# Weights split on other engines, query and key blocks stored in halves, later oT transposes in a diffusion trunk

## The chip, the cores and the metric

The kernel runs on one core of a Trainium2 chip. The metric is the device time of one execution in microseconds. Three runs of the kernel before took 1909.53, 1918.72 and 1919.75 us; their median is 1918.72.

TensorE (PE in the profile) multiplies matrices, VectorE (DVE) and ScalarE (ACT) work on elements, GpSimd (POOL) too; SyncE (SP) issues most transfers. Each engine takes its own list of instructions in order.

## The reference, cut to what matters

The reference is a two-layer trunk over 1024 latent tokens of width 1024 with 256 context tokens. Layer 0 projects the normalised tokens once and splits the result among neighbourhood attention (8 heads of 64) and a bidirectional gated DeltaNet (4 heads of 128, chunks of 64), with a gate z over both. Layer 1 is a Hyena layer with long convolutions. The part that the change touches is layer 0's projection and the DeltaNet. Per head and direction:

```
kb, vb = k * beta[..., None], v * beta[..., None]
lmat = where(strict, (kb @ k.T) * decay, 0)
sol  = triangular_solve(lmat, concat[vb, kb * exp(gc)], unit lower)   # u, w
aqk  = (q @ k.T) * decay
scan over chunks: o = exp(gc) q @ S + aqk @ (u - w @ S);  S = decayed S + k.T @ (...)
```

The neighbourhood attention needs q, k and v of 8 heads (two heads, a "pair", in one block of 128 columns), laid out so that a window of columns is contiguous.

## The kernel before, in words

Every projection is a block of 128 output columns against all 1024 inputs. Precision is held by splitting each operand into a high and a low part: a block is three matmuls (high x high, high x low, low x high) for each of 8 slices of the input and each stretch of 512 tokens (`gemm`, `gemm_steps`). `load_split` loads the raw weights [128, 8 x 128], casts them to the high part and subtracts to get the low part (line 105). Before the change the cast is ScalarE's by default (line 102) or another engine's (line 104), and the subtraction GpSimd's. Two weight buffers of each kind take turns, so a part of one block may be written when the block before the last one is finished.

`project` has two stages. In stage 1 (385 to some 726 us of the span) a scheduler orders the instructions of each engine from dependences and its own costs. `dn_front` runs for four heads: three projections (`dn_block`: k, v, q; tiles dn and wdn), a centred convolution on VectorE (dacc), transposes (ktp, vtp, qtp), the norms of k and q (rk, rr), the scaled ktm and its transpose kT, and then, for each half of the chunks and each direction, the products kk and aq, the row R of decays, and the masked matrices W and Wi; W is stored in lsc. Names like R_4_1 mean the second half of the chunks (from chunk 4 of 8) and the second direction; groups 8, 0 and 4 follow each other. I call this last part a head's tail. Its banks (pool pst) are three. `dn_substitute` inverts diagonal 32x32 blocks on GpSimd in 31 steps (tiles sub and Xb, lines 755 and 757), with W reloaded as Lb, and stores the result in xsc; `dn_tiles` loads it as X and U; `dn_levels` combines the blocks with small matmuls (y_0_0, z_0_0, y_0_0_0, ...). Substitutions 0 and 1 and the levels of head 0 are in stage 1, as are the gate blocks z 4 to 7 and, through a filler, z 0 and 1 and q, k, v of pair 0 (nq, nk, nv).

In stage 2 (to 985 us) TensorE's order is that of the program. Each head's chunks are scanned (`dn_scan`: hops of pa<-vtm, pa<-vg,ktm, pa<-S,kT and the outputs pb, oacc), with a given number of filler matmuls between the hops: q, k and v of pairs 1 to 3 and z 2 and 3. `dn_finish` normalises oacc on VectorE and defers the transposes oT and the product with z (line 926): a deferred piece is issued after so many fillers. 40 fillers (FILL_LOAD) stand ahead of the scans of heads 1 to 3.

The query and key blocks of a pair go through staging tiles nvst: high and low part of all 1024 tokens, cast and subtracted from line 515 on, stored to nq_d and nk_d at line 523. In stage 1 these tiles are the two buffers that dpad uses otherwise, in stage 2 two of their own.

## Time and profile before

| | us |
|---|---|
| median of three runs | 1918.72 |
| profiled execution | 1915.67 |
| its span | 1913.7 |
| TensorE busy | 1743.7 (91%) |
| VectorE busy | 1379.5 (72%) |
| ScalarE busy | 853.8 (45%) |
| GpSimd busy | 624.6 (33%) |

TensorE's mean granted clock is 0.953 of full speed. The profiled execution's own time is 2.0 us more than its span. A busy engine is not yet the reason for the time: what counts is where TensorE stands idle or runs at a lower clock, and what ends that. An entry such as "[5.85 <-POOL wdn_lo L105]" says that the engine stood idle for 5.85 us and that GpSimd's instruction of line 105 that writes wdn_lo ended it.

### The profile page before, as it was taken

What the parts mean: (1) busy time and instruction counts of PE and PEld (TensorE: products, weight loads), DVE (VectorE), ACT (ScalarE), POOL (GpSimd) and SP (SyncE); (2) the same over time, 40 slices, a digit from 0 to 9 for tenths busy, and PEclk for the clock granted to TensorE, in tenths of its full rate; (3) what the DMA queues carried; (4) which work ended last, traced back from release to release, by engine and by line L of the source; (5) the groups of instructions that cost most, each with busy time, mean ns of one, the idle gap of its engine ahead of it and who ended that gap; (6) DMA issues with size and microseconds to landing.
All of it is one profiled execution on the core that took longest, in us unless ns stands there. A gap on an engine that the chain in (4) does not pass through costs nothing. (4 is left out here: it accounts for less than half of the span.)

```text
span 1913.7 us, 30399 instructions
## 1 busy us (share of the span) xinstructions
PE 1743.7 (91%) x11156; PEld 1422.0 (74%) x11156; DVE 1379.5 (72%) x2786; ACT 853.8 (45%) x1851; POOL 624.6 (33%) x878
## 2 busy tenths in 40 slices
PE   6798988799987998999988999888999999999998
PEld 2466755688876786888866787677888888888776
DVE  5999988657648544655565665748898998898666
ACT  5566564445525342333343544544344444444421
POOL 0755554412395767811044301420000000000310
PEclk9799978899999998999998999999999999999999
DMA  8445544313434367534389854533442443444424
GB/s 303 162 131 142 171 159 160 121 45 108 142 104 122 128 202 230 174 103 158 142 236 236 233 172 105 181 94 81 111 121 72 101 124 81 123 111 112 126 104 135
DMA packets 132080, 271.05 MB, mean 142 GB/s; under 512 B 43946, under 2 KB 65978, under 8 KB 129883
## 3 DMA queue, kind: packets, MB, share of 16 engines
q1 hardware_dynamic: 122330, 233.45, 37.8%
q0 software_dynamic: 9600, 35.66, 9.9%
q8 instruction: 88, 1.44, 0.3%
q14 instruction: 62, 0.50, 0.1%
HBM read 193.03 MB, written 76.03 MB: 141 GB/s over the span
## 5 line engine op out<-in xcount | busy, mean ns | idle before, releaser
L116 PE MATMUL hx<-h1h,w1x_hi 128*128 128x512 f32 x256 | 101.2, 395 | 0.0
L112 PE MATMUL dn<-hh,wdn_lo 128*128 128x512 f32 (+1 forms) x256 | 95.6, 375 | 5.9 <-POOL wdn_lo L105 5.9
L116 PE MATMUL hx<-h1l,w1x_hi 128*128 128x512 f32 x256 | 100.9, 394 | 0.0
L652 DVE SCALAR_TENSOR_TENSOR dacc<-dpad,convw,dacc 128x1024 f32<-128x1024 f32 (+1 forms) x80 | 83.8, 1078 | 23.6 <-ACT dacc L650 19.3
L116 PE MATMUL hx<-h1h,w1x_lo 128*128 128x512 f32 x256 | 100.7, 393 | 0.0
L111 PE MATMUL dn<-hl,wdn_hi 128*128 128x512 f32 (+1 forms) x256 | 95.2, 372 | 0.0
L110 PE MATMUL dn<-hh,wdn_hi 128*128 128x512 f32 (+1 forms) x256 | 95.2, 372 | 0.0
L757 POOL TENSOR_TENSOR Xb<-Xb,sub 80x31 f32<-80x31 f32 (+15 forms) x124 | 86.3, 696 | 8.4
L755 POOL TENSOR_TENSOR sub<-Lb,Xb 80x31 f32<-80x31 f32 (+15 forms) x124 | 76.0, 613 | 35.0 <-DMA Lb<-lsc_d 21.0
L1051 ACT ACTIVATE pr<-pr,st 128x640 f32<-128x640 f32 (+1 forms) x64 | 51.4, 802 | 63.6 <-DVE st L1050 63.5
L112 PEld LDWEIGHTS dn<-hh,wdn_lo 128*128 128x128 f32 x256 | 49.1, 192 | 14.7 <-POOL wdn_lo L105 6.1
L1171 ACT COPY fx<-fx_ps 128x512 f32<-128x512 f32 (+1 forms) x96 | 43.5, 483 | 28.4 <-PE fx_ps L121 24.9
L116 PE MATMUL hu<-h1h,w1u_lo 128*128 128x512 f32 x128 | 51.3, 401 | 4.7 <-DMA w1u_lo<-in_w 4.7
L110 PEld LDWEIGHTS dn<-hh,wdn_hi 128*128 128x128 f32 x256 | 49.2, 192 | 7.8
L121 PE MATMUL fx_ps<-ident,ff 128*128 128x128 f32 x288 | 49.9, 300 | 5.6 <-ACT fx L1171 3.6
L111 PEld LDWEIGHTS dn<-hl,wdn_hi 128*128 128x128 f32 x256 | 49.0, 192 | 8.0 <-issue 0.5
L116 PEld LDWEIGHTS hx<-h1h,w1x_lo 128*128 128x128 f32 x256 | 48.1, 188 | 9.0
L116 PEld LDWEIGHTS hx<-h1h,w1x_hi 128*128 128x128 f32 x256 | 48.2, 188 | 8.9
L116 PEld LDWEIGHTS hx<-h1l,w1x_hi 128*128 128x128 f32 x256 | 48.1, 188 | 8.9
L156 POOL DMA_DIRECT2D w1x_lo<-in_w x16 | 13.8, 864 | 124.8 <-ACT w1x_lo L154 116.7
L1280 PE MATMUL fh<-fhh,w3s 128*128 128x512 f32 x64 | 37.2, 584 | 16.6 <-DVE fh L1282 16.5
L116 PE MATMUL hu<-h1h,w1u_hi 128*128 128x512 f32 x128 | 51.5, 402 | 0.8 <-ACT hpu L1632 0.8
(571 smaller groups left out, 5967.4 us busy)
## 6 DMA issues: line engine op xcount, KB each, us to landing
hG<-g_d SPq DMA_DIRECT2D x16, 1088.0 KB
g_d<-G SPq DMA_DIRECT2D x16, 1024.0 KB
em_w<-in_em_w SPq DMA_DIRECT2D x24, 512.0 KB
om_w<-in_om_w SPq DMA_DIRECT2D x24, 512.0 KB
wz_raw<-in_w0z SPq DMA_DIRECT2D x16, 512.0 KB
w1x_raw<-in_w SPq DMA_DIRECT2D x16, 512.0 KB
w1x_lo<-in_w POOLq DMA_DIRECT2D x16, 512.0 KB, 8.0
wdn_raw<-in_w0dn SPq DMA_DIRECT2D x12, 512.0 KB
```

The lines of the kernel that those rows point to most:

```text
L110: nc.tensor.matmul(ps, wh, xh, start=start, stop=False)
L111: nc.tensor.matmul(ps, wh, xl, start=False, stop=False)
L112: nc.tensor.matmul(ps, wl, xh, start=False, stop=stop)
L116: ins = self.nc.tensor.matmul(*args, **kw)
L121: ins = self.nc.tensor.transpose(out, x, self.ident)
L156: nc.gpsimd.dma_start(lo, src, accum_op=ALU.add)
L652: nc.vector.scalar_tensor_tensor(acc[:, t0:t0 + n], pad[:, o + j:o + j + n], cw[:, blk, j:j + 1], acc[:, t0:t0 + n], ALU.mult, ALU.add)
L755: nc.gpsimd.tensor_tensor(tv, Lb[:, j + 1:, j:j + 1].broadcast_to([80, m, c]), Xb[:, j:j + 1, 0:c].broadcast_to([80, m, c]), ALU.mult)
L757: nc.gpsimd.tensor_tensor(Xb[:, j + 1:, 0:c], Xb[:, j + 1:, 0:c], tv, ALU.subtract)
L1051: nc.scalar.activation(pr[:, :n], pr[:, :n], AF.Exp, bias=st[:, 0:1], scale=-1.0, accum_out=st[:, 1:2])
L1171: nc.scalar.copy(out[:, j0:j0 + m, :].rearrange("p a b -> p (a b)"), ps[:, :m * P])
L1280: nc.tensor.matmul(ps, ws[:, od, :], hh[:, sl], start=True, stop=False)
```

## The change

Three things change.

First, `load_split` takes an engine for the low part. The twelve dn blocks and the four z blocks of stage 1 have it subtracted by VectorE instead of GpSimd. The five filler weights of stage 1 (z 0, z 1, and q, k, v of pair 0) have the high part cast by ScalarE instead of GpSimd and the low part subtracted by VectorE. The fillers of stage 2 keep both on GpSimd.

Second, query and key blocks are staged for 512 tokens at a time. Each half is cast, subtracted and stored on its own: four stores of 256 KB per block, in runs of 64 elements (256 bytes), where two stores of 512 KB had whole rows of 1024 elements. Stage 2 has four staging tiles of 512 columns for two of 1024; in stage 1 one dpad buffer holds both parts of a half. Values are written by two copies of 256 columns instead of one of 512.

Third, the transposes oT of heads 0 to 2 are issued 60 fillers after the head's end instead of 39, which is inside the next head's scan.

```diff
-            self.split(raw, hi, lo, hi_eng=hi_eng)
+            self.split(raw, hi, lo, hi_eng=hi_eng, lo_eng=lo_eng)
...
-                self.vst = lambda: self.dtmp.tile([P, LA + 8], F32, name="nvst", tag="dpad")[:, :L]
+                def vst():
+                    t = self.dtmp.tile([P, LA + 8], F32, name="nvst", tag="dpad")
+                    return t[:, 0:512], t[:, 512:1024]
...
+                self.vst, self.wsplit = vst, {"lo_eng": nc.vector}
...
-                vs = self.pool(s2, "vs", bufs=2)
-                self.vst = lambda: vs.tile([P, L], F32, name="nvst", tag="vst")
+                vs = self.pool(s2, "vs", bufs=4)
+                self.vst = lambda: [vs.tile([P, 512], F32, name=f"nvst{i}", tag="vst") for i in range(2)]
+                self.wsplit = {"hi_eng": nc.gpsimd}
...
-        w = self.load_split(self.ap["w0z"][zb], f"wz{zb}_{ts[0]}", add=add)
+        w = self.load_split(self.ap["w0z"][zb], f"wz{zb}_{ts[0]}", add=add, lo_eng=self.nc.vector)
...
-                w = self.load_split(ap["w0na"][4 * kind + p], f"wn{kind}{p}", hi_eng=nc.gpsimd)
-                parts = [self.vst() for _ in range(1 if kind == 2 else 2)]
+                w = self.load_split(ap["w0na"][4 * kind + p], f"wn{kind}{p}", **self.wsplit)
...
+                    if t0 < L and (kind < 2 or t0 == 0):
+
+                        parts = self.vst()
...
+                        hi, lo = (x.rearrange("p (j r c) -> p r j c", j=8, c=8) for x in parts)
                         if kind == 0:
-                            nc.scalar.activation(by_columns(parts[1], t0 // 64), rows_of(ps), AF.Copy, scale=0.125)
-                            if t0:
-                                nc.vector.tensor_copy(parts[0].bitcast(F32R), parts[1])
-                                nc.vector.tensor_tensor(parts[1], parts[1], parts[0], ALU.subtract)
+                            nc.scalar.activation(lo, rows_of(ps), AF.Copy, scale=0.125)
+                            nc.vector.tensor_copy(parts[0].bitcast(F32R), parts[1])
+                            nc.vector.tensor_tensor(parts[1], parts[1], parts[0], ALU.subtract)
                         else:
-                            self.split(rows_of(ps), hi.bitcast(F32R), by_columns(parts[1], t0 // 64), nc.vector)
-                        if t0:
-                            for i in range(2):
-                                nc.sync.dma_start(dst[i, :, :L], parts[i])
+                            self.split(rows_of(ps), hi.bitcast(F32R), lo, nc.vector)
+                        for i in range(2):
+                            d = dst[i, :, :L].rearrange("p (j s x) -> p j s x", j=8, s=2)[:, :, t0 // 512, :]
+                            nc.sync.dma_start(d, parts[i].rearrange("p (j x) -> p j x", j=8))
...
-        w = self.load_split(self.ap["w0z"][zb], f"wz{zb}", hi_eng=self.nc.gpsimd)
+        w = self.load_split(self.ap["w0z"][zb], f"wz{zb}", **self.wsplit)
...
-        w = self.load_split(self.ap["w0dn"][blk], f"wdn{blk}")
+        w = self.load_split(self.ap["w0dn"][blk], f"wdn{blk}", lo_eng=nc.vector)
...
-        self.defer(FILL_LOAD[min(hd + 1, 3)] - 1, out)
+        self.defer(FILL_LOAD[min(hd + 1, 3)] + (20 if hd < 3 else -1), out)
```

The scheduler of stage 1 orders the instructions anew. Three places show how. First, TensorE in the middle of stage 1, where the first levels of head 0 (y_0_0) begin; dn_512 and dn_1024 are a value projection, kk_4 and R_4_0 belong to the tail of head 1. Before:

```order
1643 L111 MATMUL dn_1024_6037<-hl_195,wdn_hi 128x256
1644 L112 MATMUL dn_1024_6037<-hh_194,wdn_lo 128x256
1645 L116 MATMUL y_0_0_5611<-U_0_5591,X_0_5589 32x32 x12
1646 L673 MATMUL ktp_8_5126<-ident,dacc_5110 128x128 x2
1647 L116 MATMUL y_0_0_5611<-U_0_5591,X_0_5589 32x32 x8
1648 L673 MATMUL ktp_0_5132<-ident,dacc_5110 128x128 x4
```

All 24 rows of dn_1024 stand ahead of y_0_0 there. In the changed kernel TensorE has at this place:

```order
1611 L719 MATMUL kk_4_4863<-kT_4775 128x128 x4
1612 L110 MATMUL dn_512_6011<-hh_3608,wdn_hi 128x512
1613 L116 MATMUL y_0_0_5611<-U_0_5591,X_0_5589 32x32
1614 L725 MATMUL aq_4_4868<-dacc_4730,kT_4775 128x128 x4
1615 L729 MATMUL R_4_0_4873<-gT,gsel 128x512
1616 L116 MATMUL y_0_0_5611<-U_0_5591,X_0_5589 32x32 x19
1617 L111 MATMUL dn_512_6011<-hl_3609,wdn_hi 128x512
```

y_0_0 stands 32 rows earlier, ahead of the last matmuls of dn_512 and of all of dn_1024, which stood ahead of it.

Second, VectorE at the end of head 0's tail (W_4_1, whose store the first substitution waits for), before:

```order
806 L731 TENSOR_TENSOR Wi_4_1_4375<-W_4_1_4369,masks 128x512
807 L656 SCALAR_TENSOR_TENSOR dacc_4730<-dpad_4674,dacc_4730 128x1024
808 L732 TENSOR_TENSOR Wi_4_1_4375<-aq_4_4344,Wi_4_1_4375 128x512
809 L734 TENSOR_TENSOR W_4_1_4369<-W_4_1_4369,masks 128x512
810 L685 MEMSET ss_5124 128x2
811 L736 SCALAR_TENSOR_TENSOR W_4_1_4369<-kk_4_4339,beta,W_4_1_4369 128x128 x4
```

Nothing but a memset stands between the two steps of W_4_1 there. VectorE in the changed kernel:

```order
817 L739 TENSOR_TENSOR Wi_4_1_4375<-W_4_1_4369,masks 128x512
818 L740 TENSOR_TENSOR Wi_4_1_4375<-aq_4_4344,Wi_4_1_4375 128x512
819 L742 TENSOR_TENSOR W_4_1_4369<-W_4_1_4369,masks 128x512
820 L105 TENSOR_TENSOR wdn_lo<-wdn_raw,wdn_hi 128x1024
821 L744 SCALAR_TENSOR_TENSOR W_4_1_4369<-kk_4_4339,beta,W_4_1_4369 128x128 x4
822 L693 MEMSET ss_5124 128x2
823 L660 SCALAR_TENSOR_TENSOR dacc_5110<-dpad_5028,convw,dacc_5110 128x1024
```

The low part of a dn block now stands between the two steps of W_4_1. Further on, the four scalings U_0<-z_0_0 and X_0<-z_0_0 of head 0's levels, which stood behind the last step of head 1's W_4_1, now stand on VectorE as follows:

```order
879 L660 SCALAR_TENSOR_TENSOR dacc_5332<-dpad_5276,convw,dacc_5332 128x1024
880 L809 TENSOR_SCALAR U_0_5591<-z_0_0_5635 32x10x32
881 L810 TENSOR_SCALAR X_0_5589<-z_0_0_5635 32x10x32
882 L809 TENSOR_SCALAR U_0_5591<-z_0_0_5635 32x10x32
883 L810 TENSOR_SCALAR X_0_5589<-z_0_0_5635 32x10x32
884 L105 TENSOR_TENSOR wz_1_lo<-wz_1_raw,wz_1_hi 128x1024
885 L744 SCALAR_TENSOR_TENSOR W_4_0_4875<-kk_4_4863,beta,W_4_0_4875 128x128 x4
886 L739 TENSOR_TENSOR Wi_4_1_4899<-W_4_1_4893,masks 128x512
887 L693 MEMSET ss_5947 128x2
888 L664 SCALAR_TENSOR_TENSOR dacc_5332<-dpad_5276,dacc_5332 128x1024
889 L740 TENSOR_TENSOR Wi_4_1_4899<-aq_4_4868,Wi_4_1_4899 128x512
890 L742 TENSOR_TENSOR W_4_1_4893<-W_4_1_4893,masks 128x512
```

They stand ahead of a wz_lo, of the last step of head 1's W_4_0 and of its W_4_1.

Third, TensorE in the tail of head 3 at the end of stage 1; nq and nk are the fillers of pair 0. Before, the first half's second R and the second half:

```order
2097 L116 MATMUL nq_512_6857<-hl_3609,wn_hi 128x512
2098 L116 MATMUL nq_512_6857<-hh_3608,wn_lo 128x512
2099 L721 MATMUL R_0_1_6270<-gT,gsel 128x512
2100 L116 MATMUL nk_0_6895<-hh_189,wn_hi 128x512
2101 L116 MATMUL nk_0_6895<-hl_190,wn_hi 128x512
```

The R stands between 24 rows of nq and 24 of nk. And then on TensorE:

```order
2123 L116 MATMUL nk_0_6895<-hh_189,wn_lo 128x512
2124 L711 MATMUL kk_4_6288<-kT_6200 128x128 x4
2125 L717 MATMUL aq_4_6293<-dacc_6155,kT_6200 128x128 x4
2126 L721 MATMUL R_4_0_6298<-gT,gsel 128x512
2127 L721 MATMUL R_4_1_6316<-gT,gsel 128x512
2128 L116 MATMUL nk_512_6922<-hh_3608,wn_hi 128x512
```

The second half's four products stand together, behind nk_0 and ahead of nk_512. TensorE in the changed kernel:

```order
2120 L116 MATMUL nk_0_6909<-hh_189,wn_lo 128x512
2121 L719 MATMUL kk_0_6242<-kT_6200 128x128 x4
2122 L725 MATMUL aq_0_6247<-dacc_6155,kT_6200 128x128 x4
2123 L729 MATMUL R_0_0_6252<-gT,gsel 128x512
2124 L729 MATMUL R_0_1_6270<-gT,gsel 128x512
2125 L719 MATMUL kk_4_6288<-kT_6200 128x128 x4
2126 L725 MATMUL aq_4_6293<-dacc_6155,kT_6200 128x128 x4
2127 L729 MATMUL R_4_0_6298<-gT,gsel 128x512
2128 L729 MATMUL R_4_1_6316<-gT,gsel 128x512
2129 L116 MATMUL nk_512_6940<-hh_3608,wn_hi 128x512
```

Both halves of the tail now follow each other without a filler between them.

## Rows read from the trace of the kernel before

**Rows 1.** The page's first part: busy us, share of the span and instructions of each engine.

```profile
PE 1743.7 (91%) x11156; PEld 1422.0 (74%) x11156; DVE 1379.5 (72%) x2786; ACT 853.8 (45%) x1851; POOL 624.6 (33%) x878
```

**Rows 2.** The windows view of one stretch of 40 us and of two short ones behind the gaps that end at 546.41 and 622.67: length, busy us of PE, PEld, DVE, ACT and POOL with their counts, then the granted clock of TensorE, the DMA share and GB/s.

```profile
580.00:620.00 40.00, 32.23 (x403) 25.45 (x401) 36.62 (x62) 23.27 (x67) 20.88 (x27) 0.95 0.41 123
546.50:548.50 2.00, 2.00 (x5) 1.63 (x6) 0.00 (x0) 0.00 (x0) 1.84 (x3) 0.50 0.67 84
622.70:624.20 1.50, 1.50 (x5) 1.20 (x6) 0.00 (x0) 0.00 (x0) 1.50 (x2) 0.50 0.00 0
```

**Rows 3.** TensorE's waits from 385 to 985 us: who waited, for whom, us in total, times, the longest.

```profile
PE oT L121 <- DVE oacc L916: 8.8, 3, 3.7
PE z L116 <- POOL wz_hi L104: 7.6, 1, 7.6
PE dn L112 <- POOL wdn_lo L105: 5.9, 1, 5.9
PE pa L116 <- ACT vg L871: 5.4, 1, 5.4
...
PE z L112 <- POOL wz_lo L105: 0.7, 1, 0.7
```

**Rows 4.** TensorE's timeline at the gap before a dn projection. Columns: start in us, us, engine, line, operation, out<-in, shape, count, and in brackets the idle time before it and who ended it.

```profile
546.41 0.80 PE L112 MATMUL dn<-hh,wdn_lo 128*128 128x512 f32 x1 [5.85 <-POOL wdn_lo L105]
...
551.34 0.40 PE L112 MATMUL dn<-hh,wdn_lo 128*128 128x512 f32 x1
551.57 0.39 PE L110 MATMUL dn<-hh,wdn_hi 128*128 128x512 f32 x1
```

**Rows 5.** GpSimd's timeline of the same time, columns as in rows 4.

```profile
536.93 1.99 POOL L757 TENSOR_TENSOR Xb<-Xb,sub 80x231 f32<-80x231 f32 x1
...
539.72 0.70 POOL L757 TENSOR_TENSOR Xb<-Xb,sub 80x240 f32<-80x240 f32 x1
...
544.02 2.33 POOL L105 TENSOR_TENSOR wdn_lo<-wdn_raw,wdn_hi 128x1024 fp32r<-128x1024 f32 x1
```

**Rows 6.** TensorE's timeline at the gap before the filler z.

```profile
622.67 0.80 PE L116 MATMUL z<-hh,wz_hi 128*128 128x512 f32 x1 [7.58 <-POOL wz_hi L104]
...
623.69 2.33 PE L702 MATMUL kT<-ident,ktm 128*128 128x128 f32 x10
```

**Rows 7.** GpSimd's timeline there.

```profile
621.58 1.03 POOL L104 CAST wz_hi<-wz_raw 128x1024 fp32r<-128x1024 f32 x1
```

**Rows 8.** VectorE's groups from 385 to 740 us, shapes apart: count, busy us, mean ns, idle before. This one is the subtraction of a query's low part.

```profile
L518 DVE TENSOR_TENSOR nvst<-nvst 128x1024 f32<-128x1024 f32 x2 | 2.4, 1212 | 0.0
```

**Rows 9.** The steps of the first substitution on GpSimd that write Xb: ns min/median/max, first and last start in us, forms.

```profile
L757 POOL TENSOR_TENSOR Xb<-Xb,sub x31: 248/679/1986, 515.6 to 572.2; 80x31 f32<-80x31 f32 x2, 80x60 f32<-80x60 f32 x2, 80x87 f32<-80x87 f32 x2, 80x112 f32<-80x112 f32 x2
```

**Rows 10.** SyncE's timeline behind the first substitution: issue time and the time that issuing took.

```profile
572.47 0.33 SPq L759 DMA_DIRECT2D xsc_d<-Xb  x1
...
580.06 3.42 SPq L775 DMA_DIRECT2D U<-xsc_d  x7
```

**Rows 11.** TensorE's timeline at the first levels of head 0.

```profile
583.06 0.93 PE L116 MATMUL y<-U,X 32*32 32x32 f32 x24
...
590.18 1.09 PE L682 MATMUL vtp<-ident,dacc 128*128 128x128 f32 x8 [2.07 <-ACT ktm L674]
```

**Rows 12.** VectorE's timeline at four places: ktm of head 1, a step of head 1's W, the first scaling of the levels of head 0, ktm of head 2.

```profile
536.92 1.49 DVE L697 TENSOR_TENSOR ktm<-ktm,rr 128x1280 f32<-128x1280 f32 x1
...
582.90 1.12 DVE L736 SCALAR_TENSOR_TENSOR W<-kk,beta,W 128x128 f32<-128x128 f32 x4
...
589.49 0.47 DVE L801 TENSOR_SCALAR U<-z 32x320 f32<-32x320 f32 x1
...
612.65 1.49 DVE L697 TENSOR_TENSOR ktm<-ktm,rr 128x1280 f32<-128x1280 f32 x1
```

**Rows 13.** TensorE's timeline in the second half of head 3's tail.

```profile
714.16 1.06 PE L711 MATMUL kk<-kT 128*128 128x128 f32 x8
...
717.77 0.49 PE L721 MATMUL R<-gT,gsel 40*128 40x512 f32 x1 [1.23 <-ACT W L726]
```

**Rows 14.** VectorE's timeline there.

```profile
710.49 2.57 DVE L731 TENSOR_TENSOR Wi<-W,masks 128x512 f32<-128x512 f32 x1 [2.92 <-ACT W L728]
...
718.41 0.88 DVE L731 TENSOR_TENSOR Wi<-W,masks 128x512 f32<-128x512 f32 x1 [2.53 <-ACT W L728]
...
724.72 1.12 DVE L736 SCALAR_TENSOR_TENSOR W<-kk,beta,W 128x128 f32<-128x128 f32 x4
```

**Rows 15.** ScalarE's timeline at the start of stage 2.

```profile
742.03 1.07 ACT L102 CAST nvst<-nk 128x512 fp32r<-128x512 f32 x2 [10.75 <-DMA nq_d<-nvst]
```

**Rows 16.** SyncE's timeline there.

```profile
726.77 0.50 SPq L831 DMA_DIRECT2D ktm<-ktm_d  x1
...
730.24 1.09 SPq L523 DMA_DIRECT2D nq_d<-nvst  x2
```

**Rows 17.** TensorE's timeline at the oT transposes of heads 0 and 2.

```profile
807.72 1.98 PE L121 MATMUL oT<-ident,oacc 128*128 128x128 f32 x8 [3.73 <-DVE oacc L916]
...
813.98 0.60 PE L116 MATMUL pa<-S,kT 128*128 128x128 f32 x4
...
932.71 1.72 PE L121 MATMUL oT<-ident,oacc 128*128 128x128 f32 x8 [2.41 <-DVE oacc L916]
```

**Rows 18.** VectorE's timeline before oT of head 0.

```profile
806.97 1.56 DVE L916 TENSOR_TENSOR oacc<-oacc,sq 128x512 f32<-128x512 f32 x2
```

More of the change, by code (lines that the diff above doesn't have):

```diff
@@ L143, in defer, with load_split @@
         self.deferred.sort(key=lambda d: d[0])
-    def load_split(self, src, name, cols=P, hi_eng=None, add=False):
+    def load_split(self, src, name, cols=P, hi_eng=None, add=False, lo_eng=None):
         nc = self.nc
@@ L504, in fill_steps @@
                     if t0 < L:
-                        hi = by_columns(parts[0], t0 // 64)
                         if kind == 2:
-                            nc.scalar.activation(hi, rows_of(ps), AF.Copy, scale=0.5)
+                            for i in range(2):
+                                nc.scalar.activation(by_columns(parts[i], t0 // 64, 4),
+                                                     rows_of(ps)[:, :, 4 * i:4 * i + 4, :], AF.Copy, scale=0.5)
                             if t0:
                                 for j in (0, 4):
-                                    self.defer(8 + j, lambda x=parts[0], p=p, j=j:
-                                               self.v_tokens(x[:, j * P:], 4, p, j))
+                                    self.defer(8 + j, lambda x=parts[j // 4], p=p, j=j: self.v_tokens(x, 4, p, j))
                             continue
+                        hi, lo = (x.rearrange("p (j r c) -> p r j c", j=8, c=8) for x in parts)
                         if kind == 0:
-                            nc.scalar.activation(by_columns(parts[1], t0 // 64), rows_of(ps), AF.Copy, scale=0.125)
-                            if t0:
-                                nc.vector.tensor_copy(parts[0].bitcast(F32R), parts[1])
-                                nc.vector.tensor_tensor(parts[1], parts[1], parts[0], ALU.subtract)
-                        else:
-                            self.split(rows_of(ps), hi.bitcast(F32R), by_columns(parts[1], t0 // 64), nc.vector)
-                        if t0:
-                            for i in range(2):
-                                nc.sync.dma_start(dst[i, :, :L], parts[i])
+                            nc.scalar.activation(lo, rows_of(ps), AF.Copy, scale=0.125)
+                            nc.vector.tensor_copy(parts[0].bitcast(F32R), parts[1])
+                            nc.vector.tensor_tensor(parts[1], parts[1], parts[0], ALU.subtract)
+                        else:
+                            self.split(rows_of(ps), hi.bitcast(F32R), lo, nc.vector)
+                        for i in range(2):
+                            d = dst[i, :, :L].rearrange("p (j s x) -> p j s x", j=8, s=2)[:, :, t0 // 512, :]
+                            nc.sync.dma_start(d, parts[i].rearrange("p (j x) -> p j x", j=8))
                         continue
@@ L1864, in constants, with by_columns @@
     return {k: np.ascontiguousarray(np.asarray(v).astype(f32)) for k, v in out.items()}
-def by_columns(t, row=None):
-    t = t.rearrange("p (j r c) -> p r j c", r=ROWS, c=8)
+def by_columns(t, row=None, blocks=8):
+    t = t.rearrange("p (j r c) -> p r j c", j=blocks, c=8)
     return t if row is None else t[:, row:row + 8]
```

## The prediction

> **What bounds the kernel now.** I read the page first: TensorE is busy for 1743.7 of 1913.7 us [rows 1], so its matmuls stay, and only its gaps and slow stretches can be won or lost. The stretches came next: between 580 and 620 us, in the part the change touches, TensorE works 32.2 of 40 us, and VectorE is busy for 36.6 [rows 2]. The list of TensorE's waits then shows who ends the gaps [rows 3]: 7.6 us for a high part cast by GpSimd, 5.9 us for a low part subtracted by GpSimd, 8.8 us in three waits of the oT transposes, 5.4 us at the start of the first scan. These are the gaps the change aims at. A gap costs more than its length: behind the 5.85 us one the granted clock is 0.50 (1.2 instead of 2.4 GHz) from 546.5 to 548.5, and the same behind the gap that ends at 622.67 [rows 2]; at full clock matmuls of 512 columns follow each other at 0.23 us [rows 4]. Some ten of them, each 0.2 us too long, make about 2 us behind a gap of 6 to 8 us (an estimate).
>
> **Low parts off GpSimd.** In the first substitution GpSimd runs its wdn_lo only between two steps: it starts at 544.02 and takes 2.33 us, and TensorE goes on at 546.41 [rows 4, 5]. In the new order VectorE has this low part well ahead; the gap should go: 5.85 + 2.0 = 7.9 us. The second gap is alike: wz_hi runs on GpSimd at 621.58 for 1.03 us, TensorE resumes at 622.67 after 7.58 us [rows 6, 7], again at half the clock. ScalarE gets that cast, in an order that has it ahead of need: 7.58 + 2.0 = 9.6 us, and the 0.7 us for wz_lo [rows 3]. Sum of gains: 18.2 us. On VectorE a subtraction of this size takes 1.21 us [rows 8], so 21 low parts are 25 us of new VectorE work, over some 340 us; I put 1 us on PE for low parts that come late, between 0 and 5.
>
> **What is late next.** The gap at 546 stands in front of a second chain. The first substitution ends on GpSimd just past 572.2 [rows 9]; its result is stored at 572.47 and read back, the U loads being issued from 580.06 for 3.42 us [rows 10], and TensorE starts y_0_0 with them at 583.06 [rows 11]. It waits for nothing there, but only by chance: 10.6 us lie between the store and the matmul, all of them DMA. In the new order y_0_0 stands earlier, with 29 projection matmuls now behind it (5 of full width at 0.23 us, 24 of half width, by estimate half that: together 4.0 us) and one R (0.4). Without the first gap TensorE is there at 583.06 - 7.9 - 4.4 = 570.8. And the data? Four low parts leave the substitution (4 x 2.33 = 9.3 us). Its start is later: the last decay row of head 0, R_4_1, stands 15 rows lower and VectorE now does a low part between two steps of W_4_1; together about 3 us. And VectorE's subtraction is no free neighbour: beside the 1.49 us product ktm at 536.92 a GpSimd step took 1.99 us, a like one just after it 0.70 [rows 5, 12], so four low parts of 1.21 us cost the substitution between 0 and 4.8 us; I take 2.4. By the Trainium skill (SBUF — State Buffer, Who interferes with whom) a VectorE instruction with two SBUF inputs and a GpSimd one that reads SBUF exclude each other for the whole instruction; the row agrees with it, and taken to the letter it gives the upper end, 4.8. The substitution then ends at 572.2 - 9.3 + 3 + 2.4 = 568.3, the data are there 10.9 us later, at 579.2, and TensorE waits 8.4 us (between 3 and 11), plus 2.0 us at the low clock: +10.4. The levels that follow stand closer together than before (z_0_0, y_0_0_0 and z_0_0_0 have fewer projection rows between them), where 2.07 us were lost at vtp already [rows 11]: +1.5 (0 to 4).
>
> **The tail of head 3.** Before, R_0_0, R_0_1 and kk_4 had 25 and 24 matmuls of nq and nk between them; now kk_0, aq_0, both R, kk_4, aq_4, both R follow each other. kk_4 needs a bank that the second direction's W frees. The second half ran like that already: kk_4 at 714.16, VectorE's two directions from 718.41 to 725.84 [rows 13, 14], 11.7 us, beside which the products and the R hold TensorE for 2.9 us (714.16 to 717.77, less the 1.23 waited, and one R of 0.49). The same stretch now comes once more with nothing beside it: +8.8, between 0 (VectorE is done when TensorE arrives) and 10.
>
> **Halves of q and k.** Per pair VectorE and ScalarE do the same number of elements in more pieces; of the waits listed only the 5.4 us one hangs on a staging tile [rows 3]. At the start of stage 2 ScalarE's cast of nk_0 waits 10.75 us for the nq store, and pa<-vg stands behind it [rows 15, 3]. That store is issued at 730.24, behind the loads of ktm to AT from 726.77 on [rows 16]; in the new order the four half stores stand in the same place in SyncE's queue. The first half may land a microsecond or so sooner; but vg stands behind nk_512's cast too, which wants the second. No row shows a store in runs of 256 bytes (before: whole rows of 4 KB), so I bound: -1.5 to +3, taken as 0. The Trainium skill (DMA: Bandwidth & Descriptors, Specifications) asks for 512 bytes and more for full rate; by it the upper end is the nearer. Later heads have nothing waiting there.
>
> **Late oT transposes.** For head 0, oT waits 3.73 us until VectorE's product oacc (806.97 to 808.5) and then takes 1.98 us; pa<-S of the first hop comes at 813.98 [rows 17, 18]. Moved into hop 2 the transposes find oacc ready. The scan's first matmuls go up to 804, but its first S copy stands on VectorE behind that same product: done about 809.3, then pa<-S, 4.7 us sooner, and the 1.2 us of transposing at full speed come later: 3.5 to 3.7. Head 2, with a wait of 2.41 us in the same place: by the same ratio 2.8 with the slow transposes behind it. Head 1's had no wait, head 3's isn't moved. Together 6.5 us, between 0 (the two z products of VectorE delay the hop they now stand in) and 10.
>
> **Sum.** -18.2 + 1 + 10.4 + 1.5 + 8.8 + 0 - 6.5 = -3.0 us. The profiled execution took 1915.67 us (its span and 2.0 around it), 3 us under the median of the three runs, 1918.72; taken off the median: 1915.7 us.
>
> **Rivals.**
> - *The chains keep up.* The substitution starts no later, VectorE's low parts fall beside GpSimd's pauses, and head 3's VectorE work is done when TensorE arrives: y_0_0 waits 3 us at full clock, the tail 1 or 2. Then -18.2 - 6.5 + 3 + 2 + 1 = -18.7, about 1900 us. For it: in the old tail VectorE itself waits before Wi, 2.92 us at 710.49, for a W of ScalarE that waits for R [rows 14]. Against it: the U loads land just in time already.
> - *VectorE blocks (slower).* VectorE takes its list in order. Before, the scalings U<-z_0_0 come at 589.49 behind all of head 1's W [rows 12]; now they stand ahead of wz_lo, the W_4_0 and W_4_1 steps and the dacc sums, and they wait for TensorE's z_0_0, which waits for the DMA. By the numbers above z_0_0 is done near 585, so the scalings come some 3.5 us sooner than before; 6.6 us of W and dacc work (from 582.90 to 589.49 [rows 12]) then follow them, and three low parts, 3.6 us: ktm of head 2, at 612.65 before [rows 12], comes at about 619. TensorE reaches kT, 42 rows lower now (9.5 us), near 628 where it was 623.69 [rows 6]. So it decides from 9 us of further delay, in a stretch where VectorE has 3.4 of 40 us to spare [rows 2]: a z_0_0 at 590 and GpSimd's steps holding each low part up by one of their own, as the 1.99 us step shows the reverse of, would be enough. Then kT and with it all of head 3's sums push TensorE, by 12 to 18 us more than forecast: 1928 to 1934.
> - *The high part is no earlier.* If ScalarE's cast of wz_hi waits in its own queue behind tanh and copies, the 9.6 us stay: 1915.7 + 9.6 = 1925.3, no change to be told.
>
> **Chances.** The forecast's case 0.38, the chains keep up 0.33, VectorE blocks 0.19, the high part 0.10. Half a per cent, about what a measurement of this kernel can tell from no change (its three runs lie 10 us apart), is 9.6 us. Faster by more: the chains' case and a little of the forecast's own spread, 0.37; slower by more: 0.19 and the edge of the last rival, 0.21; the same: 0.42. Signs differ, so the range holds both sides, 1898 to 1930; the forecast's own is 1908 to 1923.
>
> **What would show it.** Right: no wait for wdn_lo or wz_hi on TensorE; a new wait at y_0_0 for X or U from xsc of 6 to 11 us with a slow stretch behind; a wait at kk_4 or R of head 3 of 6 to 10 us; pa<-vg still 4 to 7 us behind the nq store; no wait of oT except head 3's; a first substitution of about 50 us against 57. Wrong on the good side: y_0_0 without a wait. Wrong on the bad side: kT<-ktm or dn<-wdn_lo waiting for VectorE, or GpSimd's steps no shorter in sum.

## The result, and the profile after

The changed kernel takes 1922.17 us (median of 20 runs, 1917.03 to 1928.96), the kernel before 1917.51 in the same comparison (20 runs, 1909.53 to 1923.07): a ratio of 1.0025 [1.0015, 1.0035], 4.7 us slower where 3.0 us faster was forecast. The time lies in the range, and within half a per cent; the sign is wrong.

The first part of the changed kernel's page: busy us, share of the span and instructions of each engine.

```profile
PE 1744.5 (91%) x11156; PEld 1419.7 (74%) x11156; DVE 1399.7 (73%) x2815; ACT 858.9 (45%) x1864; POOL 572.1 (30%) x852
```

Against [rows 1] the work has moved as planned: GpSimd gives off 52.5 us, VectorE takes 20.2. TensorE's work is the same (1744.5 us busy for 1743.7), so again only gaps and slow stretches count. Its waits from 385 to 985 us (who waited, for whom, us in total, times, the longest) answer to [rows 3]:

```profile
PE R L729 <- ACT W L734: 13.3, 3, 10.6
PE y L116 <- DMA U<-xsc_d: 11.6, 1, 11.6
PE pa L116 <- DVE S L891: 3.1, 2, 2.4
PE pa L116 <- ACT vg L879: 2.8, 1, 2.8
PE nk L116 <- ACT nvst L524: 2.4, 1, 2.4
PE aq L725 <- DVE Wi L740: 2.2, 1, 2.2
...
PE oT L121 <- DVE X L810: 1.4, 2, 0.7
```

The waits for wdn_lo and wz_hi are gone, those for oacc of heads 0 and 2 as well, and vg's is halved. Head 3's wait for oacc, 2.6 us in both kernels, is only out of the list: it ends at 988.23 us now, where it ended at 982.47. Two waits of 11 us have come, and one of them, for R, was in no part of the forecast. TensorE's timeline gives the places (start, us, engine, line, operation, shape, count, and in brackets the idle time before it and who ended it):

```profile
577.58 0.28 PE L116 MATMUL y<-U,X 32*32 32x32 f32 x2 [11.62 <-DMA U<-xsc_d]
...
675.32 0.79 PE L729 MATMUL R<-gT,gsel 40*128 40x512 f32 x1 [10.56 <-ACT W L734]
...
721.57 0.49 PE L729 MATMUL R<-gT,gsel 40*128 40x512 f32 x1 [1.48 <-ACT W L734]
723.29 2.08 PE L719 MATMUL kk<-kT 128*128 128x128 f32 x8 [1.23 <-ACT W L734]
727.53 2.08 PE L725 MATMUL aq<-dacc,kT 128*128 128x128 f32 x8 [2.16 <-DVE Wi L740]
731.58 0.79 PE L729 MATMUL R<-gT,gsel 40*128 40x512 f32 x1 [1.23 <-ACT W L734]
734.75 0.80 PE L116 MATMUL nk<-hh,wn_hi 128*128 128x512 f32 x1 [2.38 <-ACT nvst L524]
...
755.36 0.75 PE L116 MATMUL pa<-vg,ktm 128*128 128x128 f32 x4 [2.82 <-ACT vg L879]
```

The windows view (length, busy us of PE, PEld, DVE, ACT and POOL, granted clock, DMA share, GB/s) shows what follows the gaps:

```profile
580.00:620.00 40.00, 37.08 (x420) 30.19 (x421) 36.39 (x54) 26.50 (x74) 13.08 (x19) 0.89 0.37 117
664.60:675.30 10.70, 0.15 (x2) 0.00 (x0) 1.73 (x2) 2.67 (x7) 0.00 (x0) 0.63 0.92 228
675.40:683.00 7.60, 7.60 (x27) 6.30 (x28) 7.56 (x8) 3.04 (x8) 3.75 (x2) 0.63 0.58 144
577.60:583.60 6.00, 6.00 (x54) 4.82 (x55) 2.42 (x2) 3.50 (x8) 0.00 (x0) 0.50 0.78 205
723.00:739.00 16.00, 9.94 (x28) 7.55 (x29) 13.11 (x28) 5.39 (x14) 14.45 (x20) 0.50 0.30 115
```

From 580 to 620 us TensorE is busy for 37.1 us, where it was 32.2 [rows 2]; but an idle stretch of 11.6 us now ends just before it, at 577.58, and the clock is 0.50 for 6.0 us behind that and for 16 us in head 3's tail. From 664.6 to 675.3 the three engines of the chain, TensorE, VectorE and ScalarE, are nearly still, while the DMA is busy; and for 7.6 us behind it the clock is 0.63.

**Where the wait for R comes from.** I follow the wait back from TensorE, one engine after another. First ScalarE, which writes W from R and so frees R's bank:

```profile
672.60 0.59 ACT L102 CAST nvst<-nk 128x512 fp32r<-128x512 f32 x1 [20.03 <-DMA nq_d<-nvst]
673.08 1.15 ACT L658 ACTIVATE dacc<-dpad,convw 128x1024 f32<-128x1024 f32 x1
674.13 1.13 ACT L734 ACTIVATE W<-R,ngc 128x128 f32<-128x128 f32 x4
```

Its cast of a key half waits 20 us for the buffer, which is free when the second half of the query has been stored. VectorE had finished that half long before:

```profile
652.16 0.90 DVE L526 TENSOR_TENSOR nvst<-nvst 128x512 f32<-128x512 f32 x1
...
673.22 0.69 DVE L105 TENSOR_TENSOR nvst<-nk,nvst 128x512 f32<-128x512 f32 x1 [16.74 <-ACT nvst L102]
```

The store stands on SyncE (start of the issue, us that issuing took):

```profile
642.91 1.56 SPq L531 DMA_DIRECT2D nq_d<-nvst  x2
658.83 0.34 SPq L767 DMA_DIRECT2D xsc_d<-Xb  x1
...
661.93 1.33 SPq L783 DMA_DIRECT2D X<-xsc_d  x3
...
665.79 1.25 SPq L531 DMA_DIRECT2D nq_d<-nvst  x2
667.13 3.91 SPq L783 DMA_DIRECT2D U<-xsc_d  x2
```

SyncE issues nothing from 644.5 to 658.8: the head of its queue is the second substitution's store, which waits for GpSimd's last step:

```profile
658.55 0.25 POOL L765 TENSOR_TENSOR Xb<-Xb,sub 80x31 f32<-80x31 f32 x1
658.86 2.04 POOL L766 COPY Lb<-Xb 80x1024 f32<-80x1024 f32 x1
```

The query's half is ready at 653.1, leaves at 665.8 and frees its buffer near 672. Of these 12.7 us until it leaves, 5.7 lie before the store of xsc; in the other 7.0 SyncE issues what stands between, above all the first loads of X, which need that store and begin 3.1 us behind it. In the kernel before, that store of xsc stood behind all stores of q and k on SyncE (issued at 680.8), and no half was stored on its own. In the changed kernel the scheduler has it ahead of the query's second half and of the key, the substitution having lost its low parts; that its costs have GpSimd done sooner than GpSimd is, is my reading of this order.

**Where the time went.** I measure two stretches on TensorE's timeline: from the first dn matmul to the first pa of head 0's scan (stage 1), and from there to the oT of head 3 (stage 2). Each stretch is from one profiled execution. The ratios are to runs of the kernel before in the same comparison, whose medians were 1917.51 us (changed), 1915.21 (e1 to e4), 1917.18 (e5 to e8) and 1917.12 (e9 to e12). One of e11's twelve runs took 9294 us; it is in the median of 1924.71, but not in the ratio.

| kernel | time, us | ratio to before | stage 1, us | stage 2, us |
|---|---|---|---|---|
| before | 1917.51 | | 349.4 | 245.9 |
| changed | 1922.17 | 1.0025 [1.0015, 1.0035] | 366.4 | 237.2 |
| e1 split alone | 1915.53 | 1.0004 [0.9988, 1.0020] | 356.8 | 241.8 |
| e2 halves alone | 1913.15 | 0.9985 [0.9971, 0.9998] | 349.5 | 241.8 |
| e3 late oT alone | 1913.28 | 0.9984 [0.9964, 1.0004] | 351.1 | 240.5 |
| e4 split and oT | 1915.15 | 1.0000 [0.9982, 1.0019] | 356.7 | 237.4 |
| e5 half stores on ScalarE's queue | 1918.14 | 0.9997 [0.9983, 1.0011] | 365.7 | 234.6 |
| e6 xsc and blocks on GpSimd's queue | 1901.31 | 0.9910 [0.9887, 0.9933] | 344.1 | 233.8 |
| e7 split for dn and z 4 to 7 only | 1927.36 | 1.0055 [1.0034, 1.0075] | 361.9 | 241.0 |
| e8 split for the fillers only | 1924.87 | 1.0034 [1.0011, 1.0057] | 357.0 | 239.3 |
| e9 before, xsc and blocks as e6 | 1932.66 | 1.0086 [1.0067, 1.0106] | 357.3 | 249.3 |
| e10 split and oT, queue as e6 | 1902.02 | 0.9930 [0.9909, 0.9950] | 345.0 | 245.0 |
| e11 xsc stores alone on GpSimd's queue | 1924.71 | 1.0040 [1.0023, 1.0057] | 362.2 | 240.0 |
| e12 three buffers dpad | 1926.34 | 1.0050 [1.0034, 1.0065] | 372.6 | 240.5 |

Stage 1 lost 17.1 us in the changed kernel and stage 2 gained 8.7.

### The profile page after: what moved, and what is told of

It is laid out like the page before. It is cut to its first block, busy times and chain, and to the rows that moved or that the text cites. A ratio compares the mean times of both kernels' runs of the same rounds, so it can differ in the third digit from the quotient of the medians.

```text
span 1920.2 us, 30456 instructions
## 1 busy us (share of the span) xinstructions
PE 1744.5 (91%) x11156; PEld 1419.7 (74%) x11156; DVE 1399.7 (73%) x2815; ACT 858.9 (45%) x1864; POOL 572.1 (30%) x852
## 5 line engine op out<-in xcount | busy, mean ns | idle before, releaser
L763 POOL TENSOR_TENSOR sub<-Lb,Xb 80x31 f32<-80x31 f32 (+15 forms) x124 | 86.8, 700 | 63.7 <-DMA Lb<-lsc_d 25.3
L660 DVE SCALAR_TENSOR_TENSOR dacc<-dpad,convw,dacc 128x1024 f32<-128x1024 f32 (+1 forms) x80 | 77.4, 995 | 34.0 <-ACT dacc L658 33.1
L765 POOL TENSOR_TENSOR Xb<-Xb,sub 80x31 f32<-80x31 f32 (+15 forms) x124 | 80.2, 647 | 9.1
L121 PE MATMUL pt<-ident,pr 128*128 128x128 f32 x304 | 47.2, 283 | 6.6 <-DVE pts L1072 4.6
```

Source lines behind the costliest of these rows:

```text
L121: ins = self.nc.tensor.transpose(out, x, self.ident)
L660: nc.vector.scalar_tensor_tensor(acc[:, t0:t0 + n], pad[:, o + j:o + j + n], cw[:, blk, j:j + 1], acc[:, t0:t0 + n], ALU.mult, ALU.add)
L763: nc.gpsimd.tensor_tensor(tv, Lb[:, j + 1:, j:j + 1].broadcast_to([80, m, c]), Xb[:, j:j + 1, 0:c].broadcast_to([80, m, c]), ALU.mult)
L765: nc.gpsimd.tensor_tensor(Xb[:, j + 1:, 0:c], Xb[:, j + 1:, 0:c], tv, ALU.subtract)
```

## The experiments

The theory, called S below: SyncE takes its queue in order; a substitution's store that waits for GpSimd holds up all that stands behind it, and with the halves the query's buffer is behind it. The rivals: the loss is in a part by itself (the split's late chain on VectorE, V below; the small stores, H below; the oT); or in the staging buffer; or in the bunched tail of head 3 (Q below).

**e1 to e4: the parts alone, and two together.** e1 keeps the engines of the split and has whole blocks and the old oT; e2 has the halves with the old engines and oT; e3 only the late oT; e4 is the changed kernel with whole blocks. Of each undone part one line: the second (undone in e1, e3, e4), the first (in e2, e3), the third (in e1, e2):

```diff
-                    return t[:, 0:512], t[:, 512:1024]
+                self.vst = lambda: self.dtmp.tile([P, LA + 8], F32, name="nvst", tag="dpad")[:, :L]
...
-                self.vst, self.wsplit = vst, {"lo_eng": nc.vector}
+                self.vst, self.wsplit = vst, {"hi_eng": nc.gpsimd}
...
-        self.defer(FILL_LOAD[min(hd + 1, 3)] + (20 if hd < 3 else -1), out)
+        self.defer(FILL_LOAD[min(hd + 1, 3)] - 1, out)
```

> The kernel before with the first part of the change alone (low parts of dn and z by VectorE, the fillers' high parts by ScalarE). Theory S (staging): the time of the changed kernel is lost where a half of q waits in SyncE's queue behind the store of the second substitution, and where this makes ScalarE and VectorE late; with whole staging tiles that place does not exist. Then this kernel waits at y_0_0 for 8 to 12 us as the changed one, has no wait of 10 us for R in the tail of head 2, and its head 3 tail, whose products again have fillers between them, waits under 5 us: 1908 to 1916 us, 2 to 9 us faster than before. Theory V (VectorE): the 16 low parts on VectorE are themselves what makes its chains late; then the R waits are here too and it takes 1924 to 1932 us.

> The kernel before with q and k staged and stored in halves alone. Theory S: in this order the half stores of q stand ahead of the second substitution's store, so they go out at once; no long wait of ScalarE for them; gaps for wdn_lo and wz_hi as before; the first wait of the first scan 2 to 4 us instead of 5.4: 1914 to 1919 us. Theory V expects the same here. A third one, that stores in runs of 256 bytes are slow in themselves, expects waits for nq_d and nk_d all over and 1922 us or more.

> The kernel before with the later oT transposes alone. All theories: the waits of oT for oacc of heads 0 and 2 (3.7 and 2.4 us) go with the slow stretches behind them, about 1 us comes back in the hops: 4 to 8 us faster than before, 1909.5 to 1913.5 us.

> The first and the third part together, no halves. Theory S: the sum of the two alone, 8 to 15 us under before: 1902 to 1910 us. Theory V: 1918 to 1926 us.

None of the parts is slower by itself: +0.04, -0.15 and -0.16%, by the ratios some 5 us faster in sum, and two of the three intervals reach 1. Together they are 0.25% slower. The halves cost nothing in stage 1 by themselves (349.5 against 349.4 us) and 9.8 us on top of the split (366.4 against 356.7 in e4). So no part is at fault; two of them together are. The split alone meets the same closed queue, SyncE issuing nothing from 645.5 to 662.3, but without the halves it is a store of W that is late behind it, and TensorE's wait (for W, before ktp) is 4.5 us instead of 10.6. Its y_0_0 waits 11.7 us like the changed kernel's, so that wait is the split's. S had not reckoned with the wait for W: e4, which has it too (4.5 us), took 1915.15 us, between S's 1902 to 1910 and V's 1918 to 1926.

**e5: the half stores of stage 1 on ScalarE's queue.**

```diff
-                            nc.sync.dma_start(d, parts[i].rearrange("p (j x) -> p j x", j=8))
+                            (nc.sync if self.pinned else nc.scalar).dma_start(d, parts[i].rearrange("p (j x) -> p j x", j=8))
```

> The changed kernel with one edit: in stage 1 the half stores of q and k are issued from ScalarE's queue instead of SyncE's; TensorE's order stays as it is. Theory S: the first half of k no longer waits 20 us on ScalarE for q's second store, since nothing in front of that store waits for the substitution; TensorE's wait of 10.6 us for R in the tail of head 2 falls under 4 us, and with it the slow stretch behind: 8 to 13 us less than the changed kernel, 1909 to 1914 us. The waits at y_0_0 (11 to 12 us) and in head 3's tail (8 us) stay. Theory V: the R wait is VectorE's, it stays, and so does the time, 1920 to 1924.

The wait for R fell from 10.6 to 7.3 us only, and the kernel is level with the one before, 0.9997 [0.9983, 1.0011]; S's 1909 to 1914 us were missed. In e5 VectorE has the half ready at 657.6, SyncE is held until its xsc store at 663.36, and yet the store that is no longer on SyncE goes out only at 667.14 (ScalarE's timeline, queue and engine):

```profile
667.14 1.60 ACTq L531 DMA_DIRECT2D nq_d<-nvst  x2
673.67 0.58 ACT L102 CAST nvst<-nk 128x512 fp32r<-128x512 f32 x1 [16.73 <-DMA nq_d<-nvst]
```

The semaphores in the trace give a reason: the DMAs of SyncE and ScalarE take eight completion semaphores in turn, and ScalarE's queue waits until 667.11 for the one that the store of Wi carries, which SyncE issued at 663.79, behind the blocked one. This is a reading of one trace; no run of its own was made for it.

**e6: the substitutions' stores and the loads of their blocks on GpSimd's queue.**

```diff
-        nc.sync.dma_start(xsc[0], Xb.rearrange("p a b -> p (a b)"))
+        nc.gpsimd.dma_start(xsc[0], Xb.rearrange("p a b -> p (a b)"))
...
-                    nc.sync.dma_start(T[d][32 * b:32 * b + 32, :, 32 * b:32 * b + 32],
+                    nc.gpsimd.dma_start(T[d][32 * b:32 * b + 32, :, 32 * b:32 * b + 32],
```

> The changed kernel with the substitutions' stores (xsc) and the loads of X and U blocks issued from GpSimd's queue; SyncE then waits for no substitution. Theory S: no store of q, k, Wi or W stands behind them any more; R wait of head 2 under 3 us. The scheduler also puts y_0_0 some 33 rows lower and spreads head 3's tail. 10 to 18 us less than the changed kernel: 1904 to 1912; less gain if 18 issues on GpSimd at about 0.9 us delay the next substitution. Theory V: 1918 or more.

1901.31 us, 0.9910 [0.9887, 0.9933]: faster than both kernels, by some 16 and 21 us, and than S's 1904 to 1912; V, at 1918 or more, is out. TensorE's waits from 385 to 985 us:

```profile
PE y L116 <- DMA U<-xsc_d: 7.5, 1, 7.5
...
PE nk L116 <- ACT nvst L524: 2.4, 1, 2.4
PE pa L116 <- ACT vg L879: 2.2, 1, 2.2
...
PE R L729 <- ACT W L734: 1.2, 1, 1.2
```

The long wait for R is gone, and stage 1 is 22.4 us shorter than the changed kernel's. Not all of that is the one wait: the scheduler laid out stage 1 anew, y_0_0 waits 4.1 us less, and in head 3's tail 3.6 us are waited instead of 8.5.

**e7, e8: half of the split.** e7 leaves the five fillers of stage 1 as before, e8 the dn blocks and z 4 to 7.

```diff
-                self.vst, self.wsplit = vst, {"lo_eng": nc.vector}
+                self.vst, self.wsplit = vst, {"hi_eng": nc.gpsimd}
```
```diff
-        w = self.load_split(self.ap["w0dn"][blk], f"wdn{blk}", lo_eng=nc.vector)
+        w = self.load_split(self.ap["w0dn"][blk], f"wdn{blk}")
```

> The changed kernel with its fillers of stage 1 split as before (both parts by GpSimd); 16 of the 21 low parts stay on VectorE, halves and oT stay. In this order the half stores of q and k stand ahead of the second substitution's store in SyncE's queue. Theory S: no R wait of 10 us though 16 low parts are VectorE's: wait at y_0_0 11 to 12 as in the changed kernel, the gap for the fillers' high part may be back (5 to 8 us): 1912 to 1920. Theory V: the R waits stay, 1919 to 1925.

> The changed kernel with the low parts of dn and z 4 to 7 back on GpSimd; only the five fillers of stage 1 are split by ScalarE and VectorE, halves and oT stay. In this order both pairs of half stores of q stand behind the second substitution's store, and that substitution, with low parts in it again, ends near 680. Theory S: the gap for wdn_lo (5.9) is back, no wait at y_0_0, and ScalarE and TensorE wait for q's stores 10 to 25 us: 1922 to 1940. Theory V: with 16 low parts off VectorE it is faster than the changed kernel by 5 us or more: under 1917.

In e7 the second substitution is late again (its store leaves at 697.75), SyncE is not held, and no long wait for R comes; but kT waits 6.2 us for VectorE's ktm, vg 5.0, and the time of 1912 to 1920 was missed: 1927.36. In e8 the wait for R is 6.2 us, the 5.9 us gap for wdn_lo is back and y_0_0 doesn't wait; its time lies in S's 1922 to 1940, its wait under S's 10 to 25. With half of the split both are slower than the kernel before. So taking R's wait away is not enough where another wait takes its place.

**e9 to e12: which store, which buffer, and the queue without the change.** e9 is the edit of e6 on the kernel before, e10 the same on e4, e11 moves the two xsc stores alone, e12 has a third buffer:

```diff
-                    t = self.dtmp.tile([P, LA + 8], F32, name="nvst", tag="dpad")
+                    t = self.dtmp.tile([P, LA + 8], F32, name="nvst", tag="dpad", bufs=3)
...
-        pad = self.dtmp.tile([P, LA + 8], F32, name=f"dpad{blk}", tag="dpad")
+        pad = self.dtmp.tile([P, LA + 8], F32, name=f"dpad{blk}", tag="dpad", bufs=3)
```

> The kernel before, with the substitutions' stores and the loads of their blocks issued from GpSimd's queue instead of SyncE's. Theory S (in the changed kernel a store of the query waits on SyncE behind a substitution's store, and moving the latter away pays because it takes that wait away): the kernel before has no wait of that kind, its gaps at wdn_lo and wz_hi stay at 5 to 6 us each, and the time is 1908 to 1916 us. Rival G (the other queue is worth its 16 us to any version): 1898 to 1904 us.

> The changed kernel without its halves, and with the substitutions' stores and block loads on GpSimd's queue. Without the halves and with SyncE's queue this was 1915.15 us, with the halves and GpSimd's queue 1901.31. Theory S: the halves cost only through SyncE's order; without them the tail of head 3 spreads over fewer fillers and the wait of 3 to 4 us for vg is back, so 1901 to 1907 us. Rival H (the halves cost by themselves, through more and smaller stores and the tail's bunching, about 9 us): 1891 to 1897 us.

> The changed kernel with the substitutions' two stores alone on GpSimd's queue, the loads of blocks left on SyncE's. Theory S: the store that blocks is the substitution's, so the second half of the query leaves when VectorE has it unless a block load that waits for that store takes its place at the head of SyncE's queue; the wait of 10.6 us for R falls under 3 us if the loads stand behind the query's stores in SyncE's order, and the time is 1902 to 1912 us; if the loads stand ahead of them the wait stays at 5 to 10 us and the time is 1914 to 1922 us. Rival Y (what GpSimd's queue gave was the earlier block of the first substitution, 11.6 to 7.5 us at y_0_0, and no more): 1916 to 1919 us with the wait for R as long as before.

> The changed kernel with three buffers of the class dpad instead of two, so that the halves of query and key do not take turns in one buffer; in this program the query's four stores stand ahead of the second substitution's store on SyncE. Theory S: the wait for R of 10.6 us and the cast's wait of 20 us are gone; the tail of head 3 stays bunched (8 to 9 us), y_0_0 waits 11 to 12 us, and the time is 1909 to 1916 us. Rival Q (the loss is in the tail's bunching, and the wait for R only brings forward what is waited for there): the wait for R goes, the tail costs as much more, and the time is 1919 to 1924 us.

*e12* is the sharpest. S as I had put it falls here: with a third buffer the query's stores leave at once, and the wait for R is still 11.2 us. What it waits for is another store in the same queue. SyncE and then ScalarE in e12:

```profile
647.15 1.61 SPq L531 DMA_DIRECT2D nq_d<-nvst  x2
666.50 0.34 SPq L767 DMA_DIRECT2D xsc_d<-Xb  x1
666.93 0.38 SPq L746 DMA_DIRECT2D lsc_d<-W  x1
```
```profile
670.02 1.14 ACT L734 ACTIVATE W<-R,ngc 128x128 f32<-128x128 f32 x4 [18.78 <-DMA lsc_d<-W]
```

SyncE issues nothing from 648.8 to 666.5, again until GpSimd is done, and now the store of W stands right behind it, so that W's buffer isn't free: the semaphore that ScalarE waits for is that store's. The buffer decides only which store is waited for; what makes it late is the closed queue. With vg and kT waiting longer too (4.8 and 6.2 us) it is slower than the changed kernel, 1926.34 us, beyond what either theory gave.

*e11* bears this out from the other side: the stores are off SyncE, but the loads of X, which wait for them, now stand at its head. SyncE is held until 668.0, for R only 2.5 us are left, two pieces in head 3's tail, and nv waits 7.1 us for a key half instead: the case that was on record as "the loads stand ahead", at 1924.71 us a little above its 1914 to 1922. Rival Y (1916 to 1919 us, the wait for R as long as before) is out.

*e10*: with the substitutions off SyncE the halves neither cost nor pay much: 0.9930 [0.9909, 0.9950] without them, 0.9910 [0.9887, 0.9933] with; in stage 1, 345.0 and 344.1 us. Beside SyncE's queue the same halves cost 9.8 us there. That is S's central claim, and rival H (about 9 us by themselves) is out.

*e9*: the queue is worth nothing by itself. The kernel before gets 0.86% slower with it, against G's 1898 to 1904 us and S's 1908 to 1916 alike. The second miss has its rows. GpSimd does its low parts in its own order, three within 12.2 us here; first GpSimd, then VectorE, ScalarE and TensorE in e9:

```profile
613.89 2.36 POOL L105 TENSOR_TENSOR wz_lo<-wz_raw,wz_hi 128x1024 fp32r<-128x1024 f32 x1
...
619.17 2.39 POOL L105 TENSOR_TENSOR wz_lo<-wz_raw,wz_hi 128x1024 fp32r<-128x1024 f32 x1
...
623.76 2.33 POOL L105 TENSOR_TENSOR wn_lo<-wn_raw,wn_hi 128x1024 fp32r<-128x1024 f32 x1
```
```profile
613.87 4.92 DVE L652 SCALAR_TENSOR_TENSOR dacc<-dpad,convw,dacc 128x1024 f32<-128x1024 f32 x1
...
623.21 3.96 DVE L652 SCALAR_TENSOR_TENSOR dacc<-dpad,convw,dacc 128x1024 f32<-128x1024 f32 x1
```
```profile
628.00 1.27 ACT L655 ACTIVATE dpad<-dacc 128x1280 f32<-128x1280 f32 x1 [18.50 <-DVE dacc L652]
```
```profile
630.28 1.96 PE L116 MATMUL z<-ys,X 64*64 64x64 f32 x16 [8.70 <-ACT ys L810]
```

Two steps of the convolution take 4.92 and 3.96 us instead of 1.28, ScalarE's tanh waits 18.5 us for the end of these sums, its copy of ys stands behind the tanh, and TensorE waits 8.7 us for ys. So the gain needs both, the substitutions off SyncE and the low parts off GpSimd: with the low parts alone off (e4, late oT included) the ratio is 1.0000, with the queue alone (e9) 1.0086, with both (e10) 0.9930.

Not tried: the changed kernel with nothing altered but SyncE's order. Another queue or buffer always moved other instructions too. How many of e6's 21 us are the closed queue alone therefore stays open; the rows give the wait's own size, below.

## Why the prediction was wrong

Term by term, what each was forecast at and what the changed kernel's rows give:

| term | forecast, us | measured, us | from |
|---|---|---|---|
| gap at wdn_lo, gap at wz_hi, wz_lo | -18.2 | -17.4 | none of the three is in the list of waits; before, 14.1 waited and half of 4.0 and 2.6 at a clock of 0.50 |
| low parts that come late | +1 | 0 | no wait for one of VectorE's |
| y_0_0 | +10.4 | +14.6 | 11.62, and half of 6.0 us at a clock of 0.50 |
| levels of head 0 | +1.5 | -0.5 | z waits 1.55 for ys, vtp's 2.07 [rows 11] is gone |
| tail of head 3 | +8.8 | +8.2 | 8.48 waited less 3.61 before; half of 9.94 us of work at 0.50, less half of 3.2 before |
| halves, at the start of stage 2 | 0 | -2.5 | vg waits 2.82 instead of 5.4 [rows 3] |
| late oT | -6.5 | -6.2 | what is left of stage 2's 8.7 without vg's 2.5 |
| R of head 2 | none | +13.4 | 10.56, and 0.37 of 7.6 us at a clock of 0.63 |
| sum | -3.0 | +9.6 | |

The slow stretches of the kernel before, by its windows view:

```profile
546.40:550.40 4.00, 3.99 (x9) 3.17 (x10) 0.00 (x0) 0.00 (x0) 3.76 (x5) 0.50 0.71 182
622.70:625.30 2.60, 2.60 (x10) 2.30 (x11) 0.00 (x0) 0.47 (x2) 2.60 (x2) 0.50 0.00 0
721.60:724.80 3.20, 3.20 (x9) 2.43 (x9) 3.16 (x8) 0.00 (x0) 2.91 (x4) 0.50 0.26 99
```

The clock's share is an estimate from the windows (work at half the clock taken as twice as long). Stage 1's terms add up to +18.3 us, where its stretch grew by 17.1. Stage 2's two terms make its -8.7 by construction, since late oT is only what was left. The two stretches together give +8.4 us. The span grew by 6.5, the head of the stretch being 2.6 us earlier in that execution, and the medians by 4.7.

**The step that failed** is the one on the halves: "of the waits listed only the 5.4 us one hangs on a staging tile", and its end, "Later heads have nothing waiting there". It looked for what the halves would do in stage 2, where a wait was already listed, and took the term as 0 between -1.5 and +3. Pair 0 of query and key is projected in stage 1. There the halves need one buffer four times in turn, and each turn needs its store out. The step read SyncE's order at 730 us and not at 650, and its list held TensorE's waits alone. In stage 1 of the kernel before, VectorE already waited 4.3 us for a store of the query (its timeline), but no wait of TensorE came of it:

```profile
676.30 1.29 DVE L105 TENSOR_TENSOR nvst<-nk,nvst 128x512 f32<-128x512 f32 x2 [4.34 <-DMA nq_d<-nvst]
```

In the changed kernel a wait of this kind is 20 us long on ScalarE and reaches TensorE. The order of SyncE in the changed program, with the second substitution's store ahead of the query's second half, could have been read beforehand. In "What is late next" I followed the first substitution's store to its matmul and never asked what stands behind the second one's on SyncE, though both leave low parts behind and both move up. Without this term the measured sum would be -3.8 us: the sign that was forecast. A smaller miss is y_0_0, 14.6 us for 10.4.

**What was right.** The gaps went, and what is late next came: y_0_0 for U from xsc (11.6 us where 6 to 11 were named, a clock of 0.50 behind it), the bunched tail (8.5 us in five waits where one of 6 to 10 was named, a size right in another shape), oT without a wait but for head 3's (two of 0.7 us beside). The first substitution ran from 514.4 to 567.0 us, 52.6 against 57 and a forecast of 50, its steps that write Xb:

```profile
L765 POOL TENSOR_TENSOR Xb<-Xb,sub x31: 246/669/1756, 515.4 to 566.7; 80x31 f32<-80x31 f32 x2, 80x60 f32<-80x60 f32 x2, 80x87 f32<-80x87 f32 x2, 80x112 f32<-80x112 f32 x2
```

The median is that of [rows 9], with the longest step still 1.76 us: VectorE's low parts hold single steps up now, as assumed.

**The rivals.** "The chains keep up" is out by the 11.6 us at y_0_0 and the tail. "VectorE blocks" gave the right side by the wrong way: kT waits for nothing long in the changed kernel. VectorE does stand still behind ScalarE for 16.7 us, but the order that holds all of them up is SyncE's. "The high part is no earlier" is out: wz_hi isn't waited for.

## What to carry over

When work is taken off an engine whose result is stored through a shared in-order queue, read that queue's new order around every store of that engine, not around the one that shows a wait: a store that is ordered too early closes the queue until its producer is done, and what waits is whatever buffer stands behind it. A second buffer then only changes who waits (e12), and another queue helps only if it takes the loads that depend on the store along (e11, e6). Parts that are each harmless alone can still cost together, so a combination is to be read as a program of its own.

## What the runs showed of the hardware that was not expected

- A GpSimd subtraction of 128 x 1024 holds VectorE up too. In e9 VectorE's convolution steps take 1.28 us from 596 to 612 us, where GpSimd subtracts no weights, and 4.44 in the mean from 613 to 627, where it subtracts three (2.33 to 2.39 us each):

```profile
L652 DVE SCALAR_TENSOR_TENSOR dacc<-dpad,convw,dacc 128x1024 f32<-128x1024 f32 x6 | 7.7, 1279 | 2.5 <-ACT dacc L650 2.5
L652 DVE SCALAR_TENSOR_TENSOR dacc<-dpad,convw,dacc 128x1024 f32<-128x1024 f32 x2 | 8.9, 4441 | 0.0
```

  I had counted only what VectorE does to GpSimd. The Trainium skill (SBUF — State Buffer, Who interferes with whom) has this rule in both directions, the one that issues first holding the other up; the rows agree with the two directions. They don't settle which goes first: both of VectorE's steps begin before the subtraction (613.87 and 613.89, 623.21 and 623.76), but beside a shorter GpSimd step (613.41 to 613.93, 623.23 to 623.79).
- Stores in runs of 256 bytes cost no time that can be seen here: the halves alone are 0.9985 [0.9971, 0.9998], and vg's wait falls from 5.4 to 3.4 us in e2. Issuing them is dearer: a query's store takes SyncE 0.53 us in the median and 4.66 at most in e2, 0.33 and 0.60 before, with twice as many stores. The Trainium skill (DMA: Bandwidth & Descriptors, Specifications) wants 512 bytes for full rate; by it the upper end of my bound was the nearer, and the measurement is on the other side.
- Issuing from GpSimd is dearer, 8 loads in 4.79 us in e6 (0.60 each) against 5 in 2.41 on SyncE in the changed kernel (0.48), and from the xsc store to y_0_0 it took 12.3 us against 10.6. The version that pays this is still the fastest.
